# One arena of 8 KB tiles for all stages, and row-tile order at the turns, in a two-layer hybrid attention trunk

## The chip, the cores and the metric

The kernel runs on one core of a Trainium2 chip. The metric is the device time of one execution in microseconds (us); lower is better. The engines are TensorE (PE; its weight loads are PEld), VectorE (DVE), ScalarE (ACT), GpSimd (POOL) and SyncE (SP), which issues the loads.

## The reference

Two layers work on x, 256 rows of 1024 values in float32. Each has a token mixer and a SwiGLU feed-forward part:

```
for l in range(DEPTH):
    sh_m, sc_m, g_m, sh_f, sc_f, g_f = split(silu(c) @ w_ada[l] + b_ada[l], 6)
    h = rms_norm(x, norm_mix[l]) * (1 + sc_m) + sh_m
    q_a, kc_a, ..., g_a, q_b, k_b, v_b, g_br = split(h @ w_in[l])
    y_a = nsa_mixer(q_a, kc_a, ...)          # sparse attention, 8 heads of 64
    y_b = moba_mixer(q_b, k_b, v_b)          # block attention, 8 heads of 64
    gate_a, gate_b = split(sigmoid(g_br), 2)
    merged = gate_a * (y_a @ w_up_nsa[l]) + gate_b * (y_b @ w_up_moba[l])
    x = x + g_m * (merged @ w_out[l])
    h = rms_norm(x, norm_ffn[l]) * (1 + sc_f) + sh_f
    gt, up = split(h @ w_ffn_in[l], 2)       # 2816 columns each
    x = x + g_f * ((silu(gt) * up) @ w_ffn_out[l])
```

## The kernel before, in words

The 256 rows are two row tiles, t=0 and t=1, of 128 rows. Each dense product is made from split operands: a value is written as hi + lo in the fp32r type, and three products hi·hi, lo·hi and hi·lo are summed in a PSUM bank (`mm3`, line 728). In the trace a product `bank<-hi,hp` or `bank<-lo,hp` has a weight tile first and a piece of the activations behind it. Some products use a whole float32 weight tile instead (`bank<-raw,...`).

**Units.** The weights come in units of up to 1 MB, 128x2048: SP loads a unit into a `raw` tile, ACT copies it to `hi` (line 438 in the profile), DVE writes `lo = raw - hi` (line 390). `load_unit` and `split_unit` (718, 696) do this. There are three raw, three hi and three lo tiles of 8 KB a partition. A raw tile is free again when lo is written, a hi and a lo tile when the last product of the unit has read them.

**Other storage.** The activations lie in 18 cells of 2 KB, handed out by a small class, `Region`, and by the kinds `pa` (mixer), `tg` (gates) and `pc0`, `pc1` (feed-forward, t=0 and t=1); in four `hd` and eight `hp` tiles of 2 KB (`hp` holds the hi and lo pieces of the normalised rows, which are transposed); and in `gbc`, the gate row that multiplies a sublayer's output. The adaLN weights of the later parts go through three `aw` tiles; DVE reduces each (line 396).

**What sets the order.** The kernel's operations are recorded first (class `Program`). A list planner then places them: it has a cost for each operation, the length of the longest path behind it (`levels`), and the free slots of every kind; for each engine it takes the ready operation of the highest rank among those that can start soonest. `ahead()` raises a group on the engines other than PE by 1000; `R.boost`, set from `HBOOST`, raises the norm and its transposes. The result is one fixed list of instructions for each engine.

**The turns.** A turn is the place where one sublayer's output becomes the next one's normalised input. For each row tile: the output products end in two banks of 512 columns; DVE multiplies by `gbc` and adds to x (line 390); ACT squares and sums (768); DVE and POOL make 1/rms by a power (POOL, line 759: `rx`); ACT or DVE scale x (780, 781); PE transposes it in eight 128x128 pieces (457); ACT and DVE apply shift and scale and make `hp` hi and lo; the next products can begin. At the mixer's output the order of the units' products is the list `TURNS` of (column half c, row half of the weights kh, row tile t); the first feed-forward products use the same list. In the feed-forward output of layer 0 the last three units' products are ordered by row tile. In the text, turn A is mixer to feed-forward of layer 0 (about 205 to 260 us), turn B feed-forward of layer 0 to mixer of layer 1 (430 to 505), turn C as A in layer 1 (620 to 680). `grpA` is the first group of mixer columns in layer 1: four units.

## Time and profile before

| what | value |
|---|---|
| median of 3 runs | 869.53 us (868.05, 869.53, 877.01) |
| the profiled execution, its own time | 865.6 us |
| its span | 863.8 us |
| mean granted clock of TensorE | 0.983 |
| DMA moved | 183.82 MB |

The profile is of one execution. Its engine table gives busy time, share of the span and number of instructions. In the waits, a row names the waiting engine and line, what it waited for, and then the time in total, how often, and the longest. In the timeline a row is start, length, engine, line, operation, out<-in and shapes; in brackets stands how long the engine had been idle before, and what released it. In a table of windows a row is a stretch, its length, the busy time of PE, PEld, DVE, ACT and POOL, the granted clock (1.00 is full), the DMA share and GB/s. In the chain of waits a row is start, length and what the end of the program was waiting for then. Buffer numbers are left out in all of these.

### The profile page before, as it was taken

What the parts mean: (1) busy time and instruction counts of PE and PEld (TensorE: products, weight loads), DVE (VectorE), ACT (ScalarE), POOL (GpSimd) and SP (SyncE); (2) the same over time, 40 slices, a digit from 0 to 9 for tenths busy, and PEclk for the clock granted to TensorE, in tenths of its full rate; (3) what the DMA queues carried; (4) which work ended last, traced back from release to release, by engine and by line L of the source; (5) the groups of instructions that cost most, each with busy time, mean ns of one, the idle gap of its engine ahead of it and who ended that gap; (6) DMA issues with size and microseconds to landing.
All of it is one profiled execution on the core that took longest, in us unless ns stands there. A gap on an engine that the chain in (4) does not pass through costs nothing.

```text
span 863.8 us, 10474 instructions
## 1 busy us (share of the span) xinstructions
PE 817.1 (95%) x3948; PEld 618.4 (72%) x3948; DVE 580.5 (67%) x1026; ACT 405.8 (47%) x644; POOL 68.0 (8%) x71
## 2 busy tenths in 40 slices
PE   7998999999879999999979999999987999999996
PEld 3667656745658878888858778776565788889885
DVE  7878877777778677877687897555337545355444
ACT  6346556633354353333364537577226543254331
POOL 5401600000000000000012121000001000000000
PEclk9999999999979999999999999999989999999999
DMA  9987474368858888889838764411265256547441
GB/s 365 402 278 248 148 267 147 123 217 303 290 166 310 317 282 311 321 312 342 288 125 268 221 218 148 145 50 36 68 238 182 70 181 205 192 146 238 153 144 49
DMA packets 75204, 183.82 MB, mean 213 GB/s; under 512 B 4113, under 2 KB 9233, under 8 KB 75154
## 3 DMA queue, kind: packets, MB, share of 16 engines
q1 hardware_dynamic: 75154, 183.16, 61.0%
q8 instruction: 31, 0.51, 0.3%
q14 instruction: 19, 0.16, 0.1%
HBM read 182.10 MB, written 1.05 MB: 212 GB/s over the span
## 4 chain that ended last, share of the span: by engine, by line
PE 81%; DMA 7%; DVE 6%; ACT 3%; issue 1%; POOL 1%; SPq 0%; DVEq 0%; ACTq 0%
PE bank L453 77%; PE bank L457 5%; DVE lo L390 3%; DMA raw<-in_w_in 2%; DMA raw<-in_w_out 2%; ACT hi L438 2%; DMA vecs<-in_vecs 1%; DMA raw<-in_w_ffn_in 1%; DVE tmp L390 1%; DMA aw<-in_w_ada 1%; POOL rx L759 1%; ACT hp L438 1%; DVE tmp L408 0%; DVE x L390 0%; DVE aw L396 0%
## 5 line engine op out<-in xcount | busy, mean ns | idle before, releaser
L453 PE MATMUL bank<-hi,hp 128*128 128x512 f32 (+2 forms) x1296 | 407.6, 388 | 7.4 <-ACT hp L438 3.9
L438 ACT ACTIVATE hi<-raw 128x2048 fp32r<-128x2048 f32 (+2 forms) x107 | 201.1, 1892 | 288.8 <-PE bank L453 207.7
L390 DVE TENSOR_TENSOR lo<-raw,hi 128x2048 fp32r<-128x2048 f32 (+2 forms) x107 | 240.0, 2264 | 122.4 <-ACT hi L438 121.9
L453 PEld LDWEIGHTS bank<-hi,hp 128*128 128x128 f32 x1296 | 241.1, 190 | 63.6 <-issue 7.2
L453 PE MATMUL bank<-lo,hp 128*128 128x512 f32 (+2 forms) x648 | 246.6, 381 | 3.3 <-DVE lo L390 3.3
L453 PEld LDWEIGHTS bank<-lo,hp 128*128 128x128 f32 x648 | 123.7, 191 | 28.6 <-DVE lo L390 5.4
L453 PE MATMUL bank<-hi,cell 128*128 128x512 f32 x416 | 138.8, 401 | 0.1
L396 DVE SCALAR_TENSOR_TENSOR aw<-aw,crow 128x1024 f32<-128x1024 f32 x80 | 95.6, 1219 | 22.4 <-DMA aw<-in_w_ada 22.3
L453 PEld LDWEIGHTS bank<-hi,cell 128*128 128x128 f32 x416 | 79.5, 191 | 17.6 <-issue 0.5
L453 PE MATMUL bank<-lo,cell 128*128 128x512 f32 x208 | 83.3, 401 | 3.2 <-DVE lo L390 3.2
L453 PE MATMUL bank<-raw,cell 128*31 128x128 f32 (+1 forms) x256 | 63.6, 438 | 2.7 <-DVE tmp L396 1.5
L457 PE MATMUL bank<-ident,tmp 128*128 128x128 f32 x256 | 40.9, 298 | 14.6 <-ACT tmp L780 8.4
L453 PE MATMUL bank<-raw,hd 128*128 128x512 f32 (+1 forms) x112 | 50.8, 585 | 1.7 <-ACT hd L438 1.7
L457 PEld LDWEIGHTS bank<-ident,tmp 128*128 128x128 f32 x256 | 32.9, 152 | 25.9 <-ACT tmp L780 10.4
L759 POOL TENSOR_TENSOR rx<-rx,mhalf 128x1 f32<-128x1 f32 x8 | 11.6, 1456 | 487.9 <-DVE rx L408 484.2
L453 PEld LDWEIGHTS bank<-lo,cell 128*128 128x128 f32 x208 | 39.8, 191 | 13.2 <-DVE lo L390 4.9
L453 PEld LDWEIGHTS bank<-raw,cell 128*31 128x31 f32 (+1 forms) x256 | 26.9, 164 | 28.3 <-issue 24.2
L402 DVE CUSTOM_DVE_ANT_0 at<-bank,maskf 128x128 f32<-128x128 f32 (+1 forms) x96 | 30.1, 352 | 23.3 <-PE bank L457 13.5
L438 ACT ACTIVATE at<-at,nb,rqa 128x128 f32<-128x128 f32 (+1 forms) x64 | 34.1, 536 | 3.3 <-DVE nb L396 3.2
L453 PEld LDWEIGHTS bank<-raw,hd 128*128 128x128 f32 x112 | 21.1, 196 | 19.0 <-issue 15.6
L438 ACT ACTIVATE cell<-bank 128x512 fp32r<-128x512 f32 (+2 forms) x44 | 24.2, 575 | 17.2 <-PE bank L453 10.4
L390 DVE TENSOR_TENSOR tmp<-tmp,bank 128x512 f32<-128x512 f32 (+1 forms) x24 | 15.1, 637 | 18.5 <-PE bank L453 18.5
(165 smaller groups left out, 676.5 us busy)
## 6 DMA issues: line engine op xcount, KB each, us to landing
raw<-in_w_ffn_in SPq DMA_DIRECT2D x44, 1024.0 KB, 6.3
aw<-in_w_ada SPq DMA_DIRECT2D x80, 512.0 KB, 5.5
raw<-in_w_in SPq DMA_DIRECT2D x30, 1024.0 KB, 5.3
raw<-in_w_ffn_out SPq DMA_DIRECT2D x22, 1024.0 KB, 5.4
sa<-in_w_ada SPq DMA_DIRECT2D x8, 1024.0 KB, 10.5
raw<-in_w_out SPq DMA_DIRECT2D x8, 1024.0 KB, 5.5
raw<-in_w_in SPq DMA_DIRECT2D x8, 908.0 KB, 8.2
raw<-in_w_up_nsa SPq DMA_DIRECT2D x4, 1024.0 KB, 5.1
```

The lines of the kernel that those rows point to most:

```text
L390: self._vec(engs, cols(out), True, lambda v: v.tensor_tensor(AP(out), AP(a), AP(b), op=op), [a, b], [out])
L396: lambda v: v.scalar_tensor_tensor(AP(out), AP(a), AP(s), AP(b), op0=op0, op1=op1, **{k: AP(x) for k, x in kw.items()}),
L402: lambda v: v.tensor_tensor_reduce(AP(out), AP(a), AP(b), 1.0, init, op0, op1, AP(accum)),
L438: self.p.op({"ACT": (c, [lambda: self.nc.scalar.activation(AP(out), AP(a), func, **{k: AP(x) for k, x in kw.items()})])}, reads, writes)
L453: self.p.op({"PE": (cost, [lambda: self.nc.tensor.matmul(AP(out), AP(lhsT), AP(rhs), start=start, stop=stop)])}, [lhsT, rhs], [out])
L457: self.p.op({"PE": (0.109, [lambda: self.nc.tensor.transpose(AP(out), AP(a), AP(ident))])}, [a, ident], [out])
L759: E_.raw("POOL", 1.1 + 0.13 * n, lambda: nc.gpsimd.tensor_tensor(AP(r), AP(r), AP(mh), op=ALU.pow), [r, mhalf], [r])
```

## The change

The change has four parts. (1) All of the storage above except the small tiles becomes one arena of 17 tiles of 8 KB, `big0` to `big16`; each kind is a list of arena tiles, and kinds of different stages share them. A kind marked `inturn` takes its tiles strictly in the order of its list. (2) `raw`, `hi` and `lo` get spare tiles (raw: 11; hi: 15 and 12; lo: 16 and 13), which only units loaded with `spare=True` may take: the four units of the mixer's output, the first units of each feed-forward part, the last four of layer 0's feed-forward output, and `grpA`. So up to five split units are live at a turn. (3) The orders at the turns change: `OUT_TURNS` at the mixer's output, `FFN_TURNS` at the first feed-forward columns (all of t=0, then all of t=1), the last four units in place of three in layer 0's feed-forward output, and `grpA` of layer 1 with all units of t=0 before those of t=1. (4) The boosts are smaller: `HBOOST` 20 and 20, with `HALF_BOOST` for the first column half.

```
 class Slot:
-    def __init__(self, ap, cells, fresh=None):
+    def __init__(self, ap, cells, fresh=None, spare=False):
...
                 for s in k.slots:
-                    if any(c.busy or id(c) in taken for c in s.cells):
+                    if any(c.busy or id(c) in taken for c in s.cells) or (s.spare and not v.spare):
                         continue
...
+                    if k.inturn:
+                        break
...
-HBOOST = (120.0, 60.0)
+HBOOST = (20.0, 20.0)
+HALF_BOOST = 20.0
...
-TURNS = [(0, 0, 0), (0, 1, 0), (1, 0, 0), (0, 0, 1), (1, 1, 0), (0, 1, 1), (1, 0, 1), (1, 1, 1)]
+OUT_TURNS = [(0, 0, 0), (1, 0, 0), (0, 0, 1), (0, 1, 0), (1, 1, 0), (1, 0, 1), (0, 1, 1), (1, 1, 1)]
+FFN_TURNS = [(c, k, t) for t in range(2) for c, k in ((0, 0), (1, 0), (0, 1), (1, 1))]
...
+    arena("raw", (0, 1, 2, 11), (11,))
+    arena("hi", (3, 4, 5, 15, 12), (15, 12))
+    arena("lo", (6, 7, 8, 16, 13), (16, 13))
+    arena("hp", (9, 10))
+    arena("hd", (11,))
+    arena("sa", (12, 13, 14, 15, 16))
+    for kind in ("e", "kk", "qq", "ve", "tg"):
+        arena(kind, (12, 13, 14, 15, 16), inturn=True)
+    arena("yy", (11, 12, 13, 14), inturn=True)
+    arena("mT", (9, 10))
+    arena("gbc", (14, 10), inturn=True)
+    arena("aT", (15, 16, 12, 13, 14, 11), inturn=True)
...
-            for c0, n, bb in ((512, 512, b1), (1024, 280, b2)):
-                for kh in range(2):
-                    u = win(c0, n, kh)
-                    for t in range(NT):
-                        if kh == 0:
-                            bb[t] = R.val("n")
-                        part(bb[t], h[t], u, 4 * kh, kh == 0, kh == 1)
+            us = [(c0, n, bb, kh, win(c0, n, kh, True)) for c0, n, bb in ((512, 512, b1), (1024, 280, b2))
+                  for kh in range(2)]
+            for t in range(NT):
+                for c0, n, bb, kh, u in us:
+                    if kh == 0:
+                        bb[t] = R.val("n")
+                    part(bb[t], h[t], u, 4 * kh, kh == 0, kh == 1)
...
-        for c in range(2):
-            for kh in range(2):
-                us[(c, kh)] = load_unit(WO[kh * 512:(kh + 1) * 512, c * 512:(c + 1) * 512], 4, 512)
-        for c, kh, t in TURNS:
+        for kh in range(2):
+            for c in range(2):
+                us[(c, kh)] = load_unit(WO[kh * 512:(kh + 1) * 512, c * 512:(c + 1) * 512], 4, 512, spare=True)
+        for c, kh, t in OUT_TURNS:
             part(bs[(c, t)], mT[t], us[(c, kh)], 4 * kh, kh == 0, kh == 1)
...
-            us.append(split_unit(raw, 2, D))
-        keys = [(i, t, k, c) for i in range(nu - 3) for t in range(NT) for k in range(2) for c in range(2)]
+            us.append(split_unit(raw, 2, D, l < L - 1 and i >= nu - 4))
+        nl = 3 if l == L - 1 else 4
+        keys = [(i, t, k, c) for i in range(nu - nl) for t in range(NT) for k in range(2) for c in range(2)]
```

What this does to the lists of instructions is shown at three places. In these rows a tile's name has the number of its slot, then of the tile; lines 450, 454, 435, 442, 729 and 741 of the changed kernel are 453, 457, 438, 445, 768 and 780 of the one before.

First PE at turn A. Before, `bank4_67` gets the last products of t=0 (the second column half), `bank2_65` those of t=1, `tmp4` and `tmp3` are t=0's scaled rows, `hp0` their first hi piece. Between the second and third group of rows nine more products of `bank2_65` stand.

```order
L453 MATMUL bank4_67<-hi2_90,cell0_1582 128x512
L453 MATMUL bank4_67<-lo2_87,cell0_1582 128x512
L453 MATMUL bank4_67<-hi2_90,cell3_1593 128x512
L453 MATMUL bank2_65<-hi2_90,cell5_1596 128x512
L453 MATMUL bank2_65<-lo2_87,cell5_1596 128x512
L453 MATMUL bank2_65<-hi2_90,cell1_1612 128x512
...
L457 MATMUL bank6_69<-ident0_123,tmp4_106 128x128 x4
L457 MATMUL bank7_70<-ident0_123,tmp3_105 128x128 x4
L453 MATMUL bank0_63<-hi1_89,hp0_94 128x512
L453 MATMUL bank0_63<-lo1_86,hp0_94 128x512
```

Now `bank3_66` and `bank4_67` are t=0's banks, `bank5_68` and `bank0_63` t=1's; before the transposes there are 27 products of t=1, and nine more behind them:

```order
L450 MATMUL bank4_67<-hi12_1623,mT9_1555 128x512
L450 MATMUL bank4_67<-lo8_1640,mT9_1555 128x512
L450 MATMUL bank4_67<-hi12_1623,mT9_1555 128x512
L450 MATMUL bank5_68<-hi3_1544,mT10_1567 128x512
L450 MATMUL bank5_68<-lo6_1552,mT10_1567 128x512
L450 MATMUL bank5_68<-hi3_1544,mT10_1567 128x512
...
L454 MATMUL bank7_70<-ident0_95,tmp4_79 128x128 x4
L454 MATMUL bank6_69<-ident0_95,tmp5_80 128x128 x4
L450 MATMUL bank0_63<-hi12_1623,mT10_1567 128x512
L450 MATMUL bank0_63<-lo8_1640,mT10_1567 128x512
L450 MATMUL bank0_63<-hi12_1623,mT10_1567 128x512
```

The end of t=0 has moved from 12 products ahead of its transposes to 27, and part of t=1 behind them.

Then ACT at turn A: the two gate rows, the squares (768), the norm (780) and the first `hp` pieces, with the splits of units among them. Before:

```order
L445 ACTIVATE gbc0_114<-bank7_70 128x512
L438 ACTIVATE hi2_90<-raw1_83 128x2048
L438 ACTIVATE hi1_89<-raw2_84 128x2048
L438 ACTIVATE hi0_88<-raw0_82 128x2048
L768 ACTIVATE tmp4_106,ssx22_152<-x00_129 128x512
L768 ACTIVATE tmp3_105,ssx22_152<-x00_129 128x512
L438 ACTIVATE hi2_90<-raw1_83 128x2048
L780 ACTIVATE tmp4_106<-x00_129,rx2_160 128x512
L438 ACTIVATE hp0_94<-bank6_69,mod_f00_164 128x128 x4
```

Now (`raw11` and `raw1` hold feed-forward units, `hi12` the fourth output unit):

```order
L435 ACTIVATE hi12_1623<-raw2_1581 128x2048
L435 ACTIVATE hi15_1642<-raw11_1584 128x2048
L442 ACTIVATE gbc14_1667<-bank7_70 128x512
L442 ACTIVATE gbc14_1667<-bank6_69 128x512
L729 ACTIVATE tmp4_79,ssx22_124<-x00_101 128x512
L729 ACTIVATE tmp5_80,ssx22_124<-x00_101 128x512
L435 ACTIVATE hi3_1716<-raw1_1612 128x2048
L741 ACTIVATE tmp4_79<-x00_101,rx2_132 128x512
L435 ACTIVATE hi4_1739<-raw0_1635 128x2048
L435 ACTIVATE hp9_1755<-bank7_70,mod_f00_136 128x128 x4
```

The first feed-forward unit's split (`hi15`) stands ahead of the gate rows; the split between squares and norm is that of the second unit, and one more has come in between norm and `hp`.

Last PE at turn C, at the second output unit. Before, `tmp1` are merged rows of t=1, `hi1`, `lo1` the third unit:

```order
L453 MATMUL bank4_67<-hi0_88,cell3_4216 128x512
L453 MATMUL bank4_67<-lo0_85,cell3_4216 128x512
L453 MATMUL bank4_67<-hi0_88,cell9_4219 128x512
L457 MATMUL bank6_69<-ident0_123,tmp1_103 128x128 x4
L453 MATMUL bank3_66<-hi1_89,cell3_4216 128x512
L453 MATMUL bank3_66<-lo1_86,cell3_4216 128x512
L453 MATMUL bank3_66<-hi1_89,cell9_4219 128x512
```

Now (`hi4`, `lo6` the second unit, `hi5`, `lo7` the third, `tmp5` the merged rows of t=1):

```order
L450 MATMUL bank3_66<-hi3_4381,mT9_4363 128x512 x2
L450 MATMUL bank3_66<-lo8_4385,mT9_4363 128x512
L450 MATMUL bank3_66<-hi3_4381,mT9_4363 128x512
L450 MATMUL bank4_67<-hi4_4418,mT9_4363 128x512
L450 MATMUL bank4_67<-lo6_4432,mT9_4363 128x512
L450 MATMUL bank4_67<-hi4_4418,mT9_4363 128x512 x2
...
L454 MATMUL bank7_70<-ident0_95,tmp5_80 128x128 x4
L450 MATMUL bank5_68<-hi3_4381,mT10_4430 128x512
...
L450 MATMUL bank3_66<-hi5_4435,mT9_4363 128x512
L450 MATMUL bank3_66<-lo7_4449,mT9_4363 128x512
```

The second unit's 12 products of t=0 have come ahead of t=1's transposes and of the third unit.

More of the change, by code (lines that the diff above doesn't have):

```diff
@@ L60, in __init__ @@
         self.hist, self.ops, self.left, self.end, self.placed = [], 0, 0, 0.0, False
-        self.tile = None
+        self.tile, self.spare = None, False
     def base(self):
@@ L157, in touch @@
             o, p, w = h
-            hit = p is None or part is None or p == part
-            if hit and (w or write) and o is not op:
+            n = min(len(p), len(part))
+            if p[:n] == part[:n] and (w or write) and o is not op:
                 op.preds[o.no] = o
-            if not (write and hit and (part is None or p == part)):
+            if not (write and p[:len(part)] == part):
                 keep.append(h)
@@ L174, in __enter__ @@
             def __enter__(self):
-                prog.first = True
+                self.was, prog.first = prog.first, prog.first or on
             def __exit__(self, *a):
-                prog.first = False
+                prog.first = self.was
         return Ahead()
@@ L261, in place @@
                     return None
-                for k2 in k.after:
-                    if any(w.left for w in k2.vals):
-                        return None
-                    t = max(t, max((w.end for w in k2.vals), default=0.0))
                 taken[id(k)] = i + 1
@@ L538, in trunk_kernel, with arena, fresh @@
         R.slots(kind, [banks[i] for i in ids], [bc[i] for i in ids], psum=True)
[L541 to L560 removed]
+    NB = 17
+    big = [Cell() for _ in range(NB)]
+    first = cp.tile([P, 2048], F32, name="big0_", tag="big0")
+    def arena(kind, ids, spare=(), inturn=False):
+        def fresh(i):
+            return lambda dt: cp.tile([P, 2048], dt, name=f"{kind}{i}", tag=f"big{i}")
+        R.kinds[kind] = Kind([Slot(first, [big[i]], fresh(i), i in spare) for i in ids], inturn=inturn)
+    arena("raw", (0, 1, 2, 11), (11,))
[10 more added lines that the diff above has]
+    arena("aT", (15, 16, 12, 13, 14, 11), inturn=True)
     tiles("aw", 3, [P, 1024])
[L562 removed]
     tiles("tmp", 6, [P, 512])
@@ L725, in load_unit @@
             return u
-        return split_unit(raw, kt, n)
+        return split_unit(raw, kt, n, spare)
     def mm3(o, xs, wh, wl, first, last):
@@ L1380, in sublayer_mix @@
         mT = [[], []]
+        mv = [R.val("mT", dt=F32R) for _ in range(NT)]
         R.stage = f"{l}ups"
@@ L1435, in post @@
                     tr(bt[:, k * P:(k + 1) * P], th[:, k * P:(k + 1) * P], ident)
-            pc = f"pc{t}"
-            hi = piece(F32R, pc)
-            hi, lo = (hi[:, :n], piece(F32R, pc)[:, :n]) if n > 256 else (hi.of(0)[:, :n], hi.of(1)[:, n:2 * n])
+            if t == 0:
+                last[0] = R.val("aT", dt=F32R)
+            hi, lo = (quarter(last[0], 2 * t + i, t, i)[:, :n] for i in range(2))
             act(hi, bt[:, :n], AF.Copy)
```

180 lines of the change are left out of this document (65 added, 115 removed).

## The prediction

> **What bounds the kernel now.** I read the page first, then the waits of TensorE, then TensorE's timeline at the three turns (the places where one sublayer hands its rows to the next), then the granted clock there, and last the chain of waits. The page:
>
> ```profile
> span 863.8 us, 10474 instructions
> PE 817.1 (95%) x3948; PEld 618.4 (72%) x3948; DVE 580.5 (67%) x1026; ACT 405.8 (47%) x644; POOL 68.0 (8%) x71
> ```
>
> TensorE is busy for 95% of the span, and the change leaves its 3532 matmuls as they are. So a gain can come from its idle time alone, and from stretches in which its clock is halved. A piece of the chain gives its full rate, 29.77/130 = 0.229 us for each product of 512 columns:
>
> ```profile
> 258.50 29.77 PE bank L453 x130
> ```
>
> The idle time is not spread out. At turn A (layer 0, mixer to feed-forward) the timeline has, with the idle time in brackets:
>
> ```profile
> 230.22 0.50 PE L453 MATMUL bank<-lo,cell 128*128 128x512 f32 x1 [0.71 <-DVE lo L390]
> 240.43 1.97 PE L457 MATMUL bank<-ident,tmp 128*128 128x128 f32 x8 [4.66 <-ACT tmp L780]
> 244.10 1.22 PE L453 MATMUL bank<-hi,hp 128*128 128x512 f32 x2 [0.79 <-DVE hp L390]
> 257.49 0.50 PE L453 MATMUL bank<-hi,hp 128*128 128x512 f32 x1 [1.76 <-ACT hp L438]
> 258.50 0.73 PE L453 MATMUL bank<-hi,hp 128*128 128x512 f32 x2 [0.27 <-DVE hp L390]
> ```
>
> That is 8.2 us. At turn C (layer 1, the same place), 9.9 us:
>
> ```profile
> 634.24 0.66 PE L457 MATMUL bank<-ident,tmp 128*128 128x128 f32 x4 [2.18 <-DVE cell L396]
> 636.43 0.80 PE L453 MATMUL bank<-lo,cell 128*128 128x512 f32 x1 [1.31 <-DVE lo L390]
> 654.87 0.50 PE L453 MATMUL bank<-lo,cell 128*128 128x512 f32 x1 [0.71 <-DVE lo L390]
> 663.67 1.97 PE L457 MATMUL bank<-ident,tmp 128*128 128x128 f32 x8 [3.26 <-ACT tmp L780]
> 667.34 0.73 PE L453 MATMUL bank<-hi,hp 128*128 128x512 f32 x2 [0.79 <-DVE hp L390]
> 677.91 0.50 PE L453 MATMUL bank<-hi,hp 128*128 128x512 f32 x1 [1.69 <-ACT hp L438]
> ```
>
> At turn B (feed-forward of layer 0 to mixer of layer 1) 4.4 us, and 1.9 us in the units behind it:
>
> ```profile
> 440.98 1.78 PE L457 MATMUL bank<-ident,tmp 128*128 128x128 f32 x8 [2.73 <-DVE tmp L781]
> 446.52 0.50 PE L453 MATMUL bank<-hi,hp 128*128 128x512 f32 x1 [0.47 <-ACT hp L438]
> 448.01 0.50 PE L453 MATMUL bank<-hi,hp 128*128 128x512 f32 x1 [0.76 <-DVE hp L390]
> 448.97 1.28 PE L457 MATMUL bank<-ident,tmp 128*128 128x128 f32 x8 [0.46 <-ACT tmp L780]
> 477.87 0.51 PE L453 MATMUL bank<-lo,hp 128*128 128x512 f32 x1 [0.91 <-DVE lo L390]
> 488.52 0.50 PE L453 MATMUL bank<-lo,hp 128*128 128x512 f32 x1 [0.94 <-DVE lo L390]
> ```
>
> The waits are paid twice. These windows (length, then PE's busy time, further on the clock) stand on the grid on which the clock changes:
>
> ```profile
> 62.40:65.80 3.40, 2.48 (x62) 2.05 (x65) 3.27 (x8) 0.68 (x2) 0.00 (x0) 1.00 0.59 218
> 65.80:69.20 3.40, 1.61 (x21) 0.98 (x13) 3.23 (x6) 2.88 (x6) 1.63 (x1) 0.99 0.52 143
> 69.20:72.60 3.40, 3.00 (x8) 2.23 (x8) 3.37 (x6) 2.08 (x4) 0.00 (x0) 0.51 1.05 404
> 243.30:246.70 3.40, 2.61 (x7) 2.14 (x7) 3.33 (x11) 1.81 (x5) 0.00 (x0) 0.50 0.94 302
> 441.30:444.70 3.40, 3.26 (x12) 2.49 (x11) 1.82 (x6) 1.35 (x4) 0.00 (x0) 0.52 0.01 2
> 635.90:639.30 3.40, 2.87 (x7) 2.29 (x8) 1.68 (x3) 0.00 (x0) 0.00 (x0) 0.50 1.02 383
> 663.20:666.60 3.40, 2.88 (x10) 2.07 (x10) 2.62 (x3) 2.19 (x7) 0.00 (x0) 0.52 0.80 269
> ```
>
> A window with 1.61 us of PE work is followed by one at half clock; one with 2.48 us is not. So the limit lies between 0.9 and 1.8 us of idle time in 3.4 us. Half clock costs half of what PE then does: at A three windows (239.9 to 250.1: 10.2 us less 0.5 and 0.8 of idle time), 4.5 us; at B one, 1.6 us; at C two and one (2.9+3.4 and 2.9 us of work), 4.6 us. The turns cost 12.7, 7.9 and 14.5 us, 35 us in all.
>
> **The change part by part.** *Turn A.* Before, row tile 0's last product of the mixer's output is followed by 12 products of row tile 1 (2.7 us) and then by row tile 0's transposes. In the change 27 products follow (6.2 us), and nine more stand behind the transposes. What must fit under this cover is the chain of row tile 0:
>
> ```profile
> 230.20 7.55 DMA raw<-in_w_ffn_in
> 239.67 0.71 ACT tmp L780
> ```
>
> These two are from the chain of waits; the timeline and the page have the rest:
>
> ```profile
> 233.78 0.69 DVE L390 TENSOR_TENSOR x<-x,tmp 128x512 f32<-128x512 f32 x1
> 234.51 0.63 ACT L768 ACTIVATE tmp<-x 128x512 f32<-128x512 f32 x1 [2.45 <-DVE x L390]
> 235.69 2.52 POOL L759 TENSOR_TENSOR rx<-rx,mhalf 128x1 f32<-128x1 f32 x1 [129.55 <-DVE rx L408]
> 237.85 1.91 ACT L438 ACTIVATE hi<-raw 128x2048 fp32r<-128x2048 f32 x1 [2.62 <-DMA raw<-in_w_ffn_in]
> L759 POOL TENSOR_TENSOR rx<-rx,mhalf 128x1 f32<-128x1 f32 x8 | 11.6, 1456 | 487.9 <-DVE rx L408 484.2
> ```
>
> Now both column halves end together: four DVE operations at about 0.65 (2.6), the second half's square 0.63+0.19, two small DVE steps 0.3, POOL 2.52, the norm 0.71: 7.0 us with no hand-over counted, against 6.2 us of cover and a first half that starts 0.7 us earlier: a wait of 0.6 us (0 to 1.5). Before, the norm was late for another reason too: on ACT the split of a feed-forward unit stood ahead of it and waited for a load that landed at 237.85, after POOL had nearly done. In the change that split still stands ahead of the norm, but its load is issued four units earlier, since a spare raw tile and two spare pairs of hi and lo hold the units; its 1.91 us then lie beside POOL's 2.52. If that load were late again, 1.4 us come back. One more split now stands between the norm and the first part; its 1.9 us lie under the transposes (1.0) and the nine products (2.1).
>
> What is late next is row tile 1. Its last product now comes just ahead of the feed-forward products. On DVE its four residual adds (2.6 us) stand ahead of the lo pieces of row tile 0's second column half: these end about 4.3 us after the first feed-forward product, which 14 products (3.2 us) cover, so PE waits 1.1 us. For row tile 1's own transposes some 2.0 us of row tile 0's parts are still in DVE's queue; then 2.6+0.8+0.3, POOL 2.0 (between its mean of 1.46 and 2.52) and 0.7: 8.4 us against 24 products (5.5 us) and that 1.1, a wait of 1.8 us, where now 1.76+0.27 are lost. Turn A after: 0.6+1.1+1.8 = 3.5 us, in windows that keep 1.6 to 2.8 us of work, so I take no halved clock. Gain 12.7−3.5 = 9.2 us (5 if one halving of three windows stays, 12.7 if all waits go).
>
> *Turn C.* The start is bound by loads:
>
> ```profile
> 624.16 5.16 DMA raw<-in_w_out
> 629.34 1.92 ACT hi L438
> 634.18 2.21 DVE lo L390
> ```
>
> The four output units are loaded at the same points as before. Before, TensorE stopped for row tile 1's transposes (2.18) and for the third unit's lo (1.31). In the change it goes on with row tile 0 and the second unit, whose lo ends at 633.5 (629.34+1.92, then 2.2 on DVE), about 1.3 us late; the third unit's lo at 636.4 and the fourth's one such operation later, near 639, come in time behind 12 and 24 products. The 1.3 us leave 2.1 us of work in that window, so the two halved windows go. Then the turn is A's: 3.5 us. After: 1.3+3.5 = 4.8 us; gain 14.5−4.8 = 9.7 us (5 to 12).
>
> *Turn B.* Row tile 0's last product is now followed by 36 products (8.2 us), but ACT's and DVE's splits of the first two mixer units stand ahead of its residual and square. From the release of the first split: ACT 1.92, DVE 2.29, four adds 2.6, the square behind ACT's second split 0.8, POOL 0.9 to 2.5, norm 0.7: 11.8 us against 11.0 us of products. Wait 0.8, then 1.2 us over the four parts, 0.95 and 0.8 at row tile 1: 3.75 us in place of 4.4+1.6. Behind it the loads get worse. The third group's four units are all held until row tile 1 has used them, and two raw tiles hold the compression weights, so the next dense units go one by one through load, hi and lo (the rows at 477.87 and 488.52 are 10.65 us apart: one such round). The first has 59 instructions of lead in place of 66, so 1.6 us more than 0.91, the second about 1.2. Also four adds of 512 columns move to POOL; none is in the trace. Nearest rows:
>
> ```profile
> L390 POOL TENSOR_TENSOR st<-vecs,nsin 128x256 f32<-128x256 f32 (+1 forms) x6 | 8.5, 1411 | 0.0
> L390 POOL TENSOR_TENSOR ct<-vecs,sincos 128x256 f32<-128x256 f32 (+1 forms) x6 | 5.4, 894 | 16.3 <-DVE tmp L390 16.3
> ```
>
> By length 1.8 to 2.8 us for one, 0.69 on DVE; two of them feed transposes ahead of that unit. I add 1.0 us (0 to 3). Turn B after: 3.75+2.5+1.2+1.0 = 8.4, from 7.9: a loss of 0.5 us (gain 2 to loss 4).
>
> *The rest.* Tiles of 8 KB taken in turn in the mixers can add waits for a former tenant; none of this is in the trace. The order shows their last readers hundreds of instructions earlier, so I take 0 (0 to 2 for each layer, by the two waits of 1.0 and 1.6 us that TensorE has on ACT there). The lead-in and the last feed-forward keep their order: 0.
>
> Sum: 9.2−0.5+9.7 = 18.4 us off the profiled execution, whose own time is 865.6: 847.2. The median of the runs, 869.5, lies 3.9 above that execution, so the forecast is 869.5−18.4 = 851.1 us.
>
> The wait that came before the halved window at 69.2 was this:
>
> ```profile
> 68.61 0.43 PE L453 MATMUL bank<-sel,at 128*128 128x60 f32 x2 [1.63 <-ACT at L438]
> ```
>
> The Trainium skill's "TensorE: Matmul & The Clock Gate" (HAM oscillation) puts the limit at an idle gap of about 3.4 us; here 1.63 us, with smaller gaps beside it, were enough, so the measurement decides. The same page (Part 4) says that transposes are not counted as busy, which speaks against this change; by that rule 0.6 us of wait and 1.0 us of transposes leave 1.8 us of counted work, inside the band that the windows leave open.
>
> **The rivals.** *The clock still falls.* If the limit is near 1.8 us of idle time, or transposes count as idle, each turn keeps a halving of one window (1.7 us) to two (3.4 us): 5 to 10 us back, 856 to 861, its middle 859. For it: window 243.3 ran at half clock though 2.61 us of work stood in it. Against: 62.4 with 2.48 us of work. Chance 0.17.
>
> *Row tile 1 takes the wait.* If none of row tile 0's parts is done on DVE by then (3.5 us of queue, not 2.0) and POOL takes 2.5, row tile 1's chain is 10.4 us against 6.6 and the wait 3.8 us: 2.0 more at each turn, and long enough to halve a window again (1.7): 3×3.7 = 11 us back, 862. For it: row tile 1's parts were late before, at 257.49 and 677.91. Against: POOL's mean is 1.46 us. Chance 0.11.
>
> *Slower: the weights starve layer 1.* The held units make each later dense unit of layer 1 wait a full round: 10.65 us against 24 products, 5.5 us, 5.2 us each. From the fourth such unit on (18.4/5.2 = 3.5) the change loses; with six of the eight units up to the values the loss is 31 us against a gain of 18: 882. For it: both rows of B's units are such rounds. Against: before, each showed under 1 us, and the leads fall by 7 to 9 instructions alone. Chance 0.07.
>
> *The change doesn't do what it says:* the spare tiles are seldom free. The order shows them used at every turn. 869, chance 0.03.
>
> **How the numbers follow.** My forecast has the remaining 0.62: 851.1, own range 841 (the waits at A and C gone) to 856 (upper ends of B). The range reaches over the clock and row tile 1: 841 to 864. About 1% can be told from no change here (869.5 ±8.7): faster is the forecast, the clock (859 is under 860.8) without a small part, and few of row tile 1's outcomes: 0.78; same 0.15; slower 0.07.
>
> **What would show it.** In the profile after: the 4.66, 3.26 and 2.73 us waits at the first transposes below 1.5; waits of 1 to 2 us at row tile 1's transposes on ACT or DVE; a mean clock of 0.99 or more, with halved windows only near 69 us and the end; the 2.18 gone and some 1.3 us on a lo at C; 2 to 4 us of waits on lo or POOL near 470 to 490. Wrong if TensorE's idle time in the turns stays above 30 us, if halved windows follow windows with over 2 us of work, or if dense units of layer 1 wait over 3 us each.

## The result, and the profile after

The changed kernel takes 848.92 us (median of 4 runs, 847.45 to 850.94), against 871.4 us (868.05 to 877.01) for the kernel before on the same chip: a ratio of 0.9737, interval 0.9677 to 0.9797. The forecast was 851.1. Of the runs below, one execution (layer 1's adds on VectorE alone, 916.48 us at a granted clock of 0.845) was a slow one and is left out, with its profile. The profiled execution of the changed kernel took 847.45 us; its page starts so:

```profile
span 845.7 us, 10445 instructions
PE 806.8 (95%) x3948; PEld 613.3 (73%) x3948; DVE 578.7 (68%) x1023; ACT 404.2 (48%) x640; POOL 73.7 (9%) x75
```

The number of matmuls is the same, 3948 on both pages (the prediction's 3532 is on neither), and TensorE's busy time fell from 817.1 to 806.8 us, its idle time from 46.7 to 38.9. The stretches at half clock add up to 27.3 us before and 17.1 us after (the end of the kernel left out in both), and the mean granted clock rose from 0.983 to 0.987; half of these 10.2 us is about 5 of the 10.3 us of busy time. The rest of it is not traced; the ends of matmuls are modelled in the profile. TensorE's timeline at the three turns, with the idle time ahead of a row in brackets, is now this (A, then B, then C):

```profile
234.79 1.03 PE L454 MATMUL bank<-ident,tmp 128*128 128x128 f32 x8
241.91 0.74 PE L450 MATMUL bank<-hi,hp 128*128 128x512 f32 x2 [0.84 <-DVE hp L387]
246.14 0.66 PE L454 MATMUL bank<-ident,tmp 128*128 128x128 f32 x4 [1.62 <-ACT tmp L741]
...
430.53 1.16 PE L454 MATMUL bank<-ident,tmp 128*128 128x128 f32 x7 [0.97 <-ACT tmp L741]
432.86 0.73 PE L450 MATMUL bank<-hi,hp 128*128 128x512 f32 x2 [0.39 <-DVE hp L387]
438.38 0.74 PE L450 MATMUL bank<-hi,hp 128*128 128x512 f32 x2 [0.43 <-DVE hp L387]
467.79 0.66 PE L454 MATMUL bank<-ident,tmp 128*128 128x128 f32 x4 [3.16 <-POOL tmp L387]
492.96 0.38 PE L450 MATMUL bank<-zb,identb 128*128 128x512 bf16 x1 [3.36 <-ACT vbd L435]
495.76 0.79 PE L450 MATMUL bank<-hi,hp 128*128 128x512 f32 x1 [2.43 <-DVE tmp L387]
...
627.37 0.50 PE L450 MATMUL bank<-lo,mT 128*128 128x512 f32 x1 [1.32 <-DVE lo L387]
645.64 1.03 PE L454 MATMUL bank<-ident,tmp 128*128 128x128 f32 x8
652.50 0.74 PE L450 MATMUL bank<-hi,hp 128*128 128x512 f32 x2 [0.58 <-DVE hp L387]
656.73 0.66 PE L454 MATMUL bank<-ident,tmp 128*128 128x128 f32 x4 [1.62 <-ACT tmp L741]
```

At A and C row tile 0's transposes (234.79, 645.64) have no bracket: nothing is waited for where 4.66 and 3.26 us were lost. Row tile 1's transposes wait 1.62 us at both. B is different: the turn itself lost most of its waits (4.4 us before, 1.8 now), and behind it stand a new one of 3.16 us and two that have grown to 3.36 and 2.43 us.

To see what each place was worth, the same event is looked up in both timelines. Before:

```profile
206.01 1.55 PE L453 MATMUL bank<-raw,cell 128*128 128x512 f32 x3 [0.58 <-DVE tmp L396]
508.95 0.27 PE L457 MATMUL bank<-ident,kbd_tok 64*128 64x64 f32 x1
609.21 1.09 PE L453 MATMUL bank<-pt,cell 128*64 128x128 f32 x14 [0.33 <-ACT pt L445]
```

After:

```profile
209.09 1.55 PE L450 MATMUL bank<-raw,yy 128*128 128x512 f32 x3 [1.68 <-DVE tmp L393]
503.50 0.27 PE L454 MATMUL bank<-ident,kbd_tok 64*128 64x64 f32 x1
602.97 1.09 PE L450 MATMUL bank<-pt,ve 128*64 128x128 f32 x14 [0.32 <-ACT pt L442]
```

So the change is 3.1 us late ahead of A, 5.4 us early behind B, 6.2 us early ahead of C and 18.1 us early at the end. In the feed-forward parts, where both kernels do the same products, the same product (by its number) comes 8.3 us earlier behind A and 17.9 us earlier behind C. So 3.1 us are lost in the lead-in and the mixer of layer 0, 11.4 gained at A, 2.9 lost at B and behind it, 0.8 gained in the mixer of layer 1, 11.6 gained at C and 0.2 in the last feed-forward.

### The profile page after: what moved, and what is told of

Read it like the earlier page. It is cut to its first block, busy times and chain, and to the rows that moved or that the text cites. A ratio compares the mean times of both kernels' runs of the same rounds, so it can differ in the third digit from the quotient of the medians.

```text
span 845.7 us, 10445 instructions
## 1 busy us (share of the span) xinstructions
PE 806.8 (95%) x3948; PEld 613.3 (73%) x3948; DVE 578.7 (68%) x1023; ACT 404.2 (48%) x640; POOL 73.7 (9%) x75
## 3 DMA queue, kind: packets, MB, share of 16 engines
HBM read 182.10 MB, written 1.05 MB: 217 GB/s over the span
## 4 chain that ended last, share of the span: by engine, by line
PE 80%; DVE 6%; DMA 6%; ACT 3%; issue 2%; POOL 1%; POOLq 0%; SPq 0%; DVEq 0%; ACTq 0%
PE bank L450 75%; PE bank L454 5%; DVE lo L387 2%; ACT hi L435 2%; DMA aw<-in_w_ada 1%; DVE tmp L387 1%; DMA raw<-in_w_out 1%; DMA vecs<-in_vecs 1%; DMA raw<-in_w_ffn_in 1%; POOL rx L720 1%; DMA raw<-in_w_in 1%; DVE x L387 1%; DVE aw L393 1%; POOL tmp L387 0%; DVE tmp L405 0%
## 5 line engine op out<-in xcount | busy, mean ns | idle before, releaser
L450 PE MATMUL bank<-hi,aT 128*128 128x512 f32 x352 | 111.0, 391 | 0.0
L450 PEld LDWEIGHTS bank<-hi,aT 128*128 128x128 f32 x352 | 66.1, 188 | 13.4
L450 PE MATMUL bank<-lo,aT 128*128 128x512 f32 x176 | 68.7, 390 | 0.0
L450 PE MATMUL bank<-raw,yy 128*128 128x512 f32 x128 | 58.6, 598 | 2.7 <-DVE tmp L393 2.6
L454 PE MATMUL bank<-ident,tmp 128*128 128x128 f32 x256 | 38.8, 284 | 8.0 <-ACT tmp L741 4.2
L454 PEld LDWEIGHTS bank<-ident,tmp 128*128 128x128 f32 x256 | 31.0, 146 | 19.1 <-ACT tmp L741 6.4
L450 PE MATMUL bank<-hi,mT 128*128 128x512 f32 x128 | 42.7, 402 | 0.0
L450 PEld LDWEIGHTS bank<-raw,yy 128*128 128x128 f32 x128 | 23.0, 190 | 26.9 <-issue 24.3
L450 PEld LDWEIGHTS bank<-lo,aT 128*128 128x128 f32 x176 | 33.1, 188 | 6.8 <-DVE lo L387 0.2
L435 ACT ACTIVATE tmp<-bank 128x512 f32<-128x512 f32 (+2 forms) x46 | 22.2, 519 | 18.9 <-PE bank L450 9.0
```

Of the source, the lines that this page charges most:

```text
L435: self.p.op({"ACT": (c, [lambda: self.nc.scalar.activation(AP(out), AP(a), func, **{k: AP(x) for k, x in kw.items()})])}, reads, writes)
L450: self.p.op({"PE": (cost, [lambda: self.nc.tensor.matmul(AP(out), AP(lhsT), AP(rhs), start=start, stop=stop)])}, [lhsT, rhs], [out])
L454: self.p.op({"PE": (0.109, [lambda: self.nc.tensor.transpose(AP(out), AP(a), AP(ident))])}, [a, ident], [out])
```

## The experiments

The theory after the result was: the gain at A and C comes from units being split further ahead, which the spare tiles allow, and from the row-tile order; the loss at B comes from the adds on POOL and from splits that stand ahead of smaller work. The rivals were that the order alone does it, or the arena alone, and that one further pair of hi and lo is enough. In the diffs + is the experiment and - the changed kernel. The kernel before took 870.6 to 871.7 us (medians) beside these runs. The changed kernel's own four runs spread over 3.5 us, so a difference of 2 us between two medians is not clear of noise.

### The old order of the output units

```
-OUT_TURNS = [(0, 0, 0), (1, 0, 0), (0, 0, 1), (0, 1, 0), (1, 1, 0), (1, 0, 1), (0, 1, 1), (1, 1, 1)]
+OUT_TURNS = [(0, 0, 0), (0, 1, 0), (1, 0, 0), (0, 0, 1), (1, 1, 0), (0, 1, 1), (1, 0, 1), (1, 1, 1)]
...
-        for kh in range(2):
-            for c in range(2):
+        for c in range(2):
+            for kh in range(2):
```

> The changed kernel with one part undone: the mixer's output products go in the old order (and its four units are loaded in the old order); arena, spare tiles and the new feed-forward order stay. Theory (the order at the output gives the gain, since it puts 27 products behind row tile 0's end and lets the second unit run ahead of the third): at turns A and C row tile 0 has about 12 products behind its end again, its transposes wait 3 to 4.5 us, at turn C the third unit is waited for again (2 to 3.5 us), and halved windows come back at both: 10 to 14 us slower than the changed kernel, 859 to 863. Rival (the spare tiles give the gain, since the splits no longer stand late ahead of the norm): under 3 us slower, at most 852.

850.77 us (848.82 to 852.38), ratio 0.9775 (0.9746 to 0.9804). Its timeline at A and at the start of C:

```profile
233.17 1.03 PE L454 MATMUL bank<-ident,tmp 128*128 128x128 f32 x8
...
628.47 0.66 PE L454 MATMUL bank<-ident,tmp 128*128 128x128 f32 x4 [2.16 <-DVE mT L393]
```

The theory that this order makes the gain fell. Row tile 0's transposes at A wait for nothing in the old order too, since the planner still puts 27 products behind row tile 0's end. What the order bought is the start of C, where the 2.16 us wait for row tile 1 is back and the changed kernel has one of 1.32 us. The times differ by 1.9 us, which the spread of the runs covers.

### The old order of the feed-forward parts

```
-FFN_TURNS = [(c, k, t) for t in range(2) for c, k in ((0, 0), (1, 0), (0, 1), (1, 1))]
+FFN_TURNS = [(0, 0, 0), (0, 1, 0), (1, 0, 0), (0, 0, 1), (1, 1, 0), (0, 1, 1), (1, 0, 1), (1, 1, 1)]
```

> The changed kernel with one part undone: the first feed-forward products go in the old order of units and row tiles; the new output order and the spare tiles stay. Theory (the old order already has three units of row tile 0, 36 products, ahead of row tile 1, so it covers row tile 1's chain as well): within 2 us of the changed kernel, 847 to 851. Rival (row tile 1's chain needs all four units of row tile 0 as cover): row tile 1's transposes wait 3 us longer at A and at C and halve a window each: 8 to 10 us slower, 857 to 859.

848.54 us (847.39 to 849.2), ratio 0.9749 (0.9725 to 0.9773): no difference from the changed kernel, as expected.

### Layer 1's adds on VectorE alone

```
-            tt(a, a, c, ALU.add, engs=("DVE", "POOL"))
+            tt(a, a, c, ALU.add, engs=("DVE",) if l else ("DVE", "POOL"))
...
```

> The changed kernel, but in layer 1 the adds of 512 columns that may go to GpSimd (of the query and key rows and of the merged rows) stay on VectorE. Theory (the 3.16 us wait near 468 us is one such add, 3.17 us long; the 3.36 and 2.43 us near 493 us come from a unit's split that stands ahead on ScalarE and VectorE, and stay, with their halved windows): 3 us faster, 845 to 846. Rival (the late add delays all that comes after it, and the waits near 493 us go with it): 9 to 12 us faster, 837 to 840. Second rival (VectorE is short there and the add only moves): no change, 848 to 850.

842.18 to 847.91 us in four runs, ratio 0.9712 (0.9673 to 0.9751): the middle of the four is about 2 us under the changed kernel, where the theory had 3, and the two intervals overlap, so a gain is not shown by these times alone. There is no trace to read here; the edit's trace is read in a later kernel that contains it.

### Layer 1's first group without row-tile order

```
-            us = [(c0, n, bb, kh, win(c0, n, kh, True)) for c0, n, bb in ((512, 512, b1), (1024, 280, b2))
-                  for kh in range(2)]
-            for t in range(NT):
-                for c0, n, bb, kh, u in us:
+            for c0, n, bb in ((512, 512, b1), (1024, 280, b2)):
+                for kh in range(2):
+                    u = win(c0, n, kh)
+                    for t in range(NT):
...
```

> The changed kernel with one part undone: the four units of layer 1's first group of columns are used by both row tiles in turn again, without spare tiles. Theory (the row-tile order there takes its gain at turn B and gives it back later, by holding the units): turn B's waits rise by 2 to 4 us (row tile 1 is needed after 12 products in place of 42), the waits between 465 and 496 us fall from 9 to 4 us and their halved window goes (3.4 us): 3 to 6 us faster, 843 to 846. Rival (turn B needs the row-tile order): turn B's waits rise by 5 us or more and halve windows: 3 to 6 us slower, 852 to 855.

854.29 us (853.01 to 855.34), ratio 0.9816 (0.979 to 0.9841): 5.4 us slower than the changed kernel. The rival's time held. Turn B in its timeline, and a row behind it:

```profile
436.12 0.73 PE L450 MATMUL bank<-hi,hp 128*128 128x512 f32 x2 [1.62 <-DVE hp L387]
441.77 0.50 PE L450 MATMUL bank<-hi,hp 128*128 128x512 f32 x1 [2.21 <-ACT hp L435]
...
509.60 0.36 PE L454 MATMUL bank<-ident,kbd_tok 64*128 64x64 f32 x1 [4.67 <-DVE kbd_tok L405]
```

Waits of 1.62 and 2.21 us stand where the changed kernel has 0.39 and 0.43. Without the order each unit is used on both row tiles at once, and TensorE comes to the next part before that part is made. In all, turn B's waits rise by 2.7 us, not by the rival's 5 or more, and one window behind 442.8 is halved. The 3.16 us on POOL went, but waits on lo of 1.21 and 1.98 us came, and the 4.67 us on `kbd_tok`; this last wait stands in three more experiments (the arena alone, all orders old, three held units) and not in the changed kernel.

### The arena without any of the rest

Here no value may take a spare slot, and all orders and the number of held units are the old ones.

```
-                    if any(c.busy or id(c) in taken for c in s.cells) or (s.spare and not v.spare):
+                    if any(c.busy or id(c) in taken for c in s.cells) or s.spare:
...
-            us.append(split_unit(raw, 2, D, l < L - 1 and i >= nu - 4))
-        nl = 3 if l == L - 1 else 4
+            us.append(split_unit(raw, 2, D, l < L - 1 and i >= nu - 3))
+        nl = 3
```

> Arena alone: the changed kernel without spare tiles (three raw, hi and lo), with the old orders at both turns, three units held in the feed-forward output of layer 0 and the old order of layer 1's first group. Theory after the first runs (the spare tiles make the gain at turns A and C: without them the fourth output unit can't be split before row tile 1 has read the first, so row tile 0 ends late, with 9 to 12 products behind it): the waits of 3 to 5 us at row tile 0's transposes and the halved windows come back at all turns: 865 to 872. Rival (the arena's way to share tiles, or the smaller boost, makes the gain): 848 to 855.

873.49 us (867.03 to 875.49, 10 runs), ratio 1.0021 (0.9995 to 1.0048): the shared arena and the smaller boosts, which stay in it, are together worth nothing and cost nothing. No run changes the boosts alone. The two large waits of before are back at A and C:

```profile
242.23 1.33 PE L454 MATMUL bank<-ident,tmp 128*128 128x128 f32 x5 [4.28 <-ACT tmp L741]
674.29 1.38 PE L454 MATMUL bank<-ident,tmp 128*128 128x128 f32 x6 [3.29 <-ACT tmp L741]
```

### Four pairs of hi and lo instead of five

```
-    arena("hi", (3, 4, 5, 15, 12), (15, 12))
-    arena("lo", (6, 7, 8, 16, 13), (16, 13))
+    arena("hi", (3, 4, 5, 15), (15,))
+    arena("lo", (6, 7, 8, 16), (16,))
```

> The changed kernel with one spare hi and one spare lo tile in place of two each (four split units live, not five). Theory (the fourth unit is what counts at turns A and C): no wait over 1.8 us at the turns' transposes, the first feed-forward unit's split comes a little later and is hidden by row tile 1's 36 products: 848 to 851. Rival (the fifth is needed, so that the next sublayer's first unit doesn't stand late ahead of the norm on ScalarE): the waits of before come back in half, 855 to 862.

861.13 us (858.12 to 862.2), ratio 0.9872 (0.982 to 0.9923). The theory that the fourth pair is enough fell: it keeps about half of the gain. Turn A in its timeline shows which half:

```profile
235.06 1.03 PE L454 MATMUL bank<-ident,tmp 128*128 128x128 f32 x8
242.26 0.73 PE L450 MATMUL bank<-hi,hp 128*128 128x512 f32 x2 [2.22 <-DVE hp L387]
246.49 1.12 PE L454 MATMUL bank<-ident,tmp 128*128 128x128 f32 x4 [3.03 <-ACT tmp L741]
```

With the fourth pair the last output unit is split before row tile 0 ends, so its transposes have their cover. But the parts and row tile 1's transposes now wait 2.22 and 3.03 us, where the changed kernel waits 0.84 and 1.62, and the clock is halved for 6.8 us behind 244.6 and again behind 664.5. The rival's time held (855 to 862), but its reason did not: ScalarE's norm of row tile 1 starts at 245.71 us, against 245.36 in the changed kernel, so it is hardly later. What is missing is work for TensorE: ahead of the first of these waits it has 8 feed-forward products where the changed kernel has 14, ahead of the second 4 in place of 10. Six products are 1.4 us, which is what each wait grew by. The fifth pair is what feeds TensorE while the chains of both row tiles run.

### All spare tiles, all orders old

> The changed kernel with spare tiles for the output's units and the first feed-forward units, but all orders as before: old order at both turns, three units held in layer 0's feed-forward output, layer 1's first group in turn. Theory (A and C live on the spare tiles, B on the row-tile order of the first group): A and C as in the changed kernel, B as before but for the smaller boosts: 2 us from the output order, 5 to 6 from the group: 854 to 858. Rival (the orders help each other, so that all of them undone lose more than the parts): 862 or more.

The diff is that of the three order experiments and of the held units together. 859.78 us (856.95 to 864.88), ratio 0.9874 (0.9821 to 0.9928), between theory and rival. Against the arena alone (873.49) the spare tiles give 13.7 us; the orders give the other 10.9 us to 848.92. Undone one at a time, the orders cost 1.9, nothing and 5.4 us, 7.3 in all. The remaining 3.6 us are no more than the spread of this run's times, so it is not shown that the orders help each other. The new orders without the spare tiles were not run.

### No adds on POOL, and the vbd copies ahead of the splits

```
-                    act(vbd[u][pr, g * 64:(g + 1) * 64], b2[pr, 64:], AF.Copy)
+                    with R.ahead(l == 1):
+                        act(vbd[u][pr, g * 64:(g + 1) * 64], b2[pr, 64:], AF.Copy)
```

The edit of the adds shown above goes with it. It was aimed at these rows of ScalarE and VectorE in the changed kernel's timeline:

```profile
489.69 1.91 ACT L435 ACTIVATE hi<-raw 128x2048 fp32r<-128x2048 f32 x1 [0.25 <-ACT vbd L435]
492.24 0.67 ACT L435 ACTIVATE vbd<-bank 32x64 f32<-32x64 f32 x3
...
491.63 2.29 DVE L387 TENSOR_TENSOR lo<-raw,hi 128x2048 fp32r<-128x2048 f32 x1 [1.21 <-ACT hi L435]
```

A split of a unit that nothing needs yet (1.91 us on ScalarE, 2.29 on VectorE) stands ahead of copies of 0.2 us each for which TensorE waits at 492.96.

> Layer 1's adds of 512 columns kept on VectorE as in the third run, and ScalarE's four small copies behind the compression raised ahead of the splits. Theory (the wait of 3.36 us near 493 us is a split of 1.9 us standing ahead of those copies, the 2.43 us behind it a lo of 2.3 us ahead of the reads of a bank): 3 us from the add, 3.4 us from the copies and 1.7 to 3.4 us from the halved window, 839 to 842. Rival (the copies only wait for something else, and the rest of the order moves the wait): as the third run, 845 to 848.

845.67 us (843.68 to 846.8), ratio 0.9703 (0.9661 to 0.9746): 3.2 us less than the changed kernel, and the lowest median of all, though its interval overlaps that of the adds alone (0.9673 to 0.9751) and that of the changed kernel (0.9677 to 0.9797). In its timeline:

```profile
466.09 0.50 PE L450 MATMUL bank<-lo,hp 128*128 128x512 f32 x1 [1.38 <-DVE lo L387]
492.80 0.77 PE L450 MATMUL bank<-hi,hp 128*128 128x512 f32 x1 [4.74 <-DVE tmp L387]
...
488.81 1.91 ACT L435 ACTIVATE hi<-raw 128x2048 fp32r<-128x2048 f32 x1
```

The rival held. The 3.16 us on POOL became 1.38 us on a lo. The wait near 493 did not go: 3.36+2.43 us became one of 4.74 us, on VectorE's rotation, and the split on ScalarE still stands ahead of what is needed.

### The rotations ahead too

The next kernel puts the squares and rotations of layer 1's three 512-column groups in the same `R.ahead(l == 1)`.

> As the eighth run (layer 1's adds on VectorE, the four copies raised), and in layer 1 the squares, sums and rotations of query and key rows are raised ahead of the splits too, on ScalarE and VectorE. Theory (the 4.74 us wait near 493 us in the eighth run is a bank that PE wants back, whose copy on ScalarE stands behind a split of 1.9 us and whose reads on VectorE come after it): that wait and its halved windows (3.4 us) go: 836 to 840. Rival (the splits put behind become late themselves, and PE waits for lo in their place): 843 to 848.

848.48 us (844.38 to 849.65), ratio 0.9732 (0.9691 to 0.9773): not better. The wait near 493 fell from 4.74 to 2.17 us, but six smaller ones (0.25 to 0.69 us) stand between 507 and 605 us, five of which the eighth run does not have. A wait on a lo at 322 us in layer 0 (2.17 us, with a halved window) is not the edit's: the eighth run has it too (2.72 us at 319.72). In layer 1 the work moved, and the waits with it. It is left open whether an order exists that removes this one.

### The power on POOL taken twice

This tests the price of the rival "row tile 1 takes the wait", by making the chain of each row tile longer on POOL. The first result goes to a scratch tile and is not used.

```
...
+        if tag == "rx":
+            E_.raw("POOL", 1.1 + 0.13 * n, lambda: (nc.gpsimd.tensor_tensor(AP(spare_r), AP(r), AP(mh), op=ALU.pow),
+                                                    nc.gpsimd.tensor_tensor(AP(r), AP(r), AP(mh), op=ALU.pow)), [r, mhalf], [r])
...
```

> The changed kernel with the power on GpSimd that ends each 1/rms done twice (the first result is thrown away), in the same order of instructions: 1.5 to 2.5 us more in each row tile's chain at each turn. Theory (row tile 0's chain is covered with about 0.5 us to spare, row tile 1's is on the path with its 1.6 us wait): row tile 0's transposes wait 1 to 2 us and row tile 1's 3 to 4 us, and some of the turns halve a window: 8 to 16 us slower, 857 to 865. Rival (the products behind cover more than that, as the missing wait at row tile 0's transposes suggests): only row tile 1 shows it, 3 to 6 us slower, 852 to 855.

861.65 us (860.09 to 862.36), ratio 0.9889 (0.9854 to 0.9924): 12.7 us slower than the changed kernel. In its timeline at A, TensorE, POOL and VectorE:

```profile
249.62 1.11 PE L454 MATMUL bank<-ident,tmp 128*128 128x128 f32 x4 [3.85 <-ACT tmp L747]
...
244.09 2.52 POOL L723 TENSOR_TENSOR spare_r<-rx,mhalf 128x1 f32<-128x1 f32 x1 [9.27 <-DVE rx L405]
246.68 2.13 POOL L724 TENSOR_TENSOR rx<-rx,mhalf 128x1 f32<-128x1 f32 x1
...
243.92 4.48 DVE L387 TENSOR_TENSOR lo<-raw,hi 128x2048 fp32r<-128x2048 f32 x2
```

The two windows there (length, then PE's busy time, further on the clock), laid where this trace's clock changes:

```profile
244.72:248.13 3.41, 1.05 (x5) 0.54 (x3) 3.41 (x2) 0.64 (x1) 3.33 (x2) 1.00 0.17 22
248.13:251.55 3.42, 1.93 (x7) 1.74 (x8) 1.06 (x4) 1.33 (x2) 0.68 (x1) 0.50 0.99 369
```

Row tile 1's wait grows by 2.2 us, to 3.85, and behind a window with 1.05 us of work the clock halves. Row tile 0's transposes still wait for nothing at A and C, as the rival had it; at B it is row tile 0 that waits, 2.20 us in place of 0.97. So the theory had the time right, and half of the reason. In the profiled execution TensorE's idle time is 7.0 us longer than in the changed kernel and its busy time, for the same matmuls, 7.9 us longer; the halved stretches go from 17.1 to 41.0 us. So about half of the loss is the clock. The prediction's rival "row tile 1 takes the wait" thus has a real mechanism at A and C. That its price (862) is also the time measured here is in part luck, since two of the added halved windows lie behind waits at 475.88 and 502.55 us that the changed kernel has too (467.79 and 492.96). In the changed kernel the window at this place holds 1.78 us of work and is not followed by a halved one.

### Three held units instead of four, and no spare raw tile

```
-            us.append(split_unit(raw, 2, D, l < L - 1 and i >= nu - 4))
-        nl = 3 if l == L - 1 else 4
+            us.append(split_unit(raw, 2, D, l < L - 1 and i >= nu - 3))
+        nl = 3
```

> The changed kernel with three in place of four units held for row-tile order in layer 0's feed-forward output (24 products of row tile 1 behind row tile 0's end in place of 36). Theory (turn B's chain of row tile 0 takes about 11 us from the release of the first split and needs the 36 products): its transposes wait 3 us longer and a window is halved: 4 to 6 us slower, 853 to 855. Rival (the chain is shorter, and its wait of 1 us comes from something else): within 1 us, 848 to 850.

```
-    arena("raw", (0, 1, 2, 11), (11,))
+    arena("raw", (0, 1, 2))
```

> The changed kernel without the spare raw tile, but with two spare hi and lo tiles. Theory (the spare raw tile only lets the first feed-forward unit land early, and three raw tiles turn over fast enough, since a raw tile is free when its lo is written): 848 to 851. Rival (with the load later its split stands late ahead of the norm on ScalarE, as in the kernel before, where it waited for a landing at 237.85): the norm at A and C is 1.5 to 3 us later, with halved windows, 853 to 858.

Three held units: 847.53 us (846.83 to 850.42), ratio 0.9736 (0.9699 to 0.9772). No spare raw tile: 849.59 us (849.12 to 854.97), ratio 0.9773 (0.9722 to 0.9824). Neither differs from the changed kernel. The theory that turn B needs 36 products behind row tile 0 fell: with fewer, its timeline still has the same 0.97 us.

```profile
436.77 1.16 PE L454 MATMUL bank<-ident,tmp 128*128 128x128 f32 x7 [0.97 <-ACT tmp L741]
```

The 3.16 us on POOL is gone there, and the wait of 4.67 us on `kbd_tok` stands 68 us later, at 504.58.

## Why the prediction was right, and where it was not

The forecast was 851.1 and the time 848.92; the sum was 18.4 us and the two profiled executions differ by 18.15. The medians on the same chip differ by 22.5 us: all four runs of the kernel before took longer than its profiled execution (865.6). That the sum came out so close is luck, since its parts were off by more than the whole: A and C gained 4.1 us more than forecast, the lead-in and B took 5.5 us more.

- **Turn A** was to gain 9.2 us and gained 11.4. Of the three waits that were to be left, 0.6 at row tile 0's transposes is 0, 1.1 on the last part's lo is 0.84 (on hp), and 1.8 at row tile 1's transposes is 1.62. So 2.46 us in place of 3.5 explain 10.2 of the 11.4; the other 1.2 are not traced. In the term of row tile 0, POOL's power took 1.46 us, not the 2.52 put in: 1.06 us less, which is more than the 0.6. That 0.6 is also more than its own terms give: a chain of 7.0 us that starts 0.7 us earlier under a cover of 6.2 us leaves 0.1.
- **The clock at A and C** was to stay full, and did. The rival that it falls there is wrong for these turns. The sign that was named for it, a mean clock of 0.99 or more with halved windows only near 69 us and the end, did not come: the mean is 0.987, and halved stretches stand at 15.6, 70.2 and 493.4 us.
- **Turn C** was to gain 9.7 us and gained 11.6. The wait on the second unit's lo, predicted 1.3, measured 1.32. With the others, 0.58 and 1.62 us, that makes 3.52 in place of 4.8.
- **Turn B** is the step that failed. It was to lose 0.5 us and lost 2.9, with other terms than predicted. The waits in the turn itself are 0.97+0.39+0.43 = 1.8 us, not 3.75. Row tile 0's 0.8 looks right beside the 0.97, but the terms of its chain add up to 9.2 to 10.8 us, not to 11.8, and by them nothing would have been waited for under the 11.0 us of products. The 2.5+1.2 us on the weights' lo did not come. An add on POOL was bounded at 1.8 to 2.8 us and its effect set at 1.0; it took 3.17 us, and TensorE waited 3.16. And the waits near 493 had no term at all. They stood in the trace before, small:

```profile
502.18 0.38 PE L453 MATMUL bank<-zb,identb 128*128 128x512 bf16 x1 [1.01 <-ACT vbd L438]
503.26 0.50 PE L453 MATMUL bank<-hi,hp 128*128 128x512 f32 x1 [0.71 <-DVE tmp L390]
```

  These 1.72 us grew to 3.36+2.43 = 5.8 us. In the changed kernel's rows a split that now comes earlier stands ahead of them; but the eighth run, which put the copies ahead of it, still waits 4.74 us there, so how much of the growth is the split's is open. The windows of the changed kernel show that the clock was lost as well:

```profile
490.00:493.41 3.41, 0.38 (x1) 0.00 (x0) 2.09 (x3) 3.31 (x6) 0.00 (x0) 1.00 1.04 410
493.41:496.83 3.42, 1.06 (x3) 0.88 (x4) 3.38 (x6) 0.12 (x1) 0.00 (x0) 0.50 0.66 168
496.83:500.24 3.41, 3.41 (x10) 2.63 (x9) 3.31 (x9) 0.60 (x1) 0.01 (x1) 0.50 0.59 229
```

  Half of 1.06+3.41 us is 2.2 us. So B now costs 1.8+3.2+5.8+2.2 = 13.0 us against 7.9+1.7 = 9.6 before: a loss of 3.4, where the same event behind B shows 2.9. Waits of about 1 us on an engine whose queue is about to be reordered should have had a term of their own.
- **The lead-in** and the mixer of layer 0 were set at 0 and lost 3.1 us. Halved stretches stand at 15.6 and 70.2 us (10.2 us in all, 3.4 before), and the wait at 209 us is 1.1 us longer than before (1.68 in place of 0.58). No run was made on this part: open.
- **The rivals.** "The weights starve layer 1" did not happen: between 430 and 610 us no dense unit waits for its lo. "Spare tiles seldom free" is wrong: they give 13.7 us. "Row tile 1 takes the wait" did not happen; the run with the power taken twice shows its mechanism at A and C.
- **What the prediction credited.** It put A's gain on the cover of 27 products. The cover is there, but the new order is not what makes it: the old order has it too, and a fourth live pair of hi and lo gives it.

## What to carry to other kernels

Where an engine stands idle at a hand-over, count the independent work that is ready to run there before looking at its order: here more split units that could be live at once gave 13.7 us with the old orders, and the new orders 10.9 us on top of that. When work is pulled ahead on an engine, list the small operations that now stand behind it: here a split of 1.9 us ahead of copies of 0.2 us stood at the largest waits that were left, though moving the copies alone took away only 1 us. And a wait that leaves a window of the clock half empty is paid twice.
